# Long-before-short product pairs in an input projection, and two activation tiles moved to multiples of 64 bytes

## The chip, the core and the metric

The kernel runs on one core of one Trainium2 chip. The metric is the device time of one execution in microseconds (us), as the median of several runs. A core has a matrix engine (PE, with its weight loads shown apart as PEld), a vector engine (DVE), a scalar engine (ACT), GpSimd (POOL), a queue engine (SP) that issues DMAs here, an on-chip memory of 128 partitions (SBUF) and an accumulator memory of eight banks (PSUM), each of which holds 512 fp32 columns in every partition.

## The reference

One encoder layer on 256 tokens of width 2048. The tokens are normed and projected by one 2048 x 18432 matrix into nine parts of 2048 columns; five of them feed a bidirectional gated linear recurrence with 16 heads (group A), four feed a gated width-3 convolution (group B). Both outputs are projected together, then a gated 256-wide embedding is added, and the result is normed.

```python
hn = rmsnorm(x, norm_w)
proj = hn @ w_in                      # 2048 x 18432
q, v, f_fwd, f_bwd, z_a, b_gate, c_gate, h_b, z_b = split(proj)
o_a = hgrn2_bidirectional(silu(q), v, f_fwd, f_bwd, lb)       # chunks of 64
o_a = head_rmsnorm(o_a, hgrn_norm_w) * silu(z_a)
o_b = rmsnorm(b_gate * conv3(c_gate * h_b), conv_norm_w) * silu(z_b)
h = x + concat([o_a, o_b]) @ w_out    # 4096 x 2048
h = h + (p @ w_ple) * sigmoid(h @ w_ple_gate)                 # 2048 x 2048
return rmsnorm(h, final_norm_w)
```

Everything is fp32.

## The kernel before

**Split products.** Every operand of the four large products is written as a high part (rounded to the format fp32r, which PE multiplies in one pass here) and a low part (the rest). A product of two operands is then three products: high by high, high by low, low by high. `Stream` loads the weights as they are, in DMAs of up to 1 MB on SP's queue, into three `raw` buffers, and `split` makes the two parts in one of five `spl` buffers: ACT writes the high part (L69) and DVE the low part (L70). The splits run three buffers ahead of the products.

**The input projection.** 72 blocks, each of 256 output columns, in the order in which the program is written: first 40 for group A (eight rounds of forward gate, backward gate, q, z, v), then 32 for group B (eight rounds of c, h, b, z). A block has two accumulators `a`, one PSUM bank each (m = 0 and 1), and 16 slices `kt` of the 2048 rows. For each slice and each accumulator `gemm_part` issues a pair of products. The *long* one has 512 moving columns: the stationary operand is a high part, the moving one is the high and the low part side by side, so that both halves of the bank are written. The *short* one has 256 moving columns: the stationary operand is the low part, the moving one the high part, and it adds to the first half of the bank. With `token_major` (the z and v of group A) the stationary operand is the activation `xs` and the moving one the weights `spl`; otherwise it is the other way about. For `kt == 0` the long product goes first (L284, L285), because it starts both halves of the bank; for all later slices the short one goes first (L287) and the long one second (L288).

**What stands between the products.** While group A's blocks run, the recurrence of the round before is done on DVE, ACT and POOL, with small products on PE. These are put between two calls of `gemm_part` by `at` and `tick`, a hand-written clock that counts calls: scores and state products (`scps`, `cx`; L459, L501), outputs (`o`; L511, L512), and the transposes `ogt` of a finished head (L359), whose result ACT and DVE write to `mixa`. The last of them fall in the fourth of group B's blocks. After that nothing but pairs stands in PE's queue until the input projection ends. Group B's gated result is written to `mixb`.

**The output projection and the gate.** `gemm_tok` multiplies `mixa` and `mixb` (stationary) by `w_out` (moving) into `pa` and `pb`: for each slice and accumulator three products of 512 columns, L630 and L631 with the high part of the activations and L632 with their low part. The same function then multiplies the transposed sum `ht` by the gate's weights into `pg` (512 columns, at the end 256), and `pt` by the embedding's weights into `pp`.

**Where the tiles lie.** Pools are filled from the low end (left) and from the high end (right) of a partition. `const` is at the left with many small tiles, each rounded up to 32 bytes; `raw`, `spl` and `xs` follow it, and `ht` takes the place of `xs`. `mixa` is the first tile of the right side; the recurrence's working tiles (`ap`) and later `mixb` are placed below it. In the built program `mixa` starts at byte 196,576 of a partition and `mixb` at 163,808, both 32 past a multiple of 64, and with them all working tiles of the recurrence but a few of the smallest. `xs`, `ht` and `pt` and all `spl` buffers start at multiples of 64.

Of the kernel before, what the change touches and what calls it, by code (L numbers as in the profile page):

```python
# [8 lines left out]
F32 = mybir.dt.float32  # L9
F32R = mybir.dt.float32r  # L10
# [7 lines left out]
P = 128  # L18
D = 2048
T = 256  # L20
NKT = D // P
NH = 16
# [58 lines left out]
def tile_hymba_encoder(  # L81
# [15 lines left out]
    act, dve, pool, pe = nc.scalar, nc.vector, nc.gpsimd, nc.tensor  # L97
    out2 = out[0].rearrange("(m p) d -> p m d", p=P)

    const = ctx.enter_context(tc.tile_pool(name="const", bufs=1))  # L100
# [6 lines left out]
    xp = xctx.enter_context(tc.tile_pool(name="xp", bufs=1, side="left"))  # L107
    mctx = ExitStack()
    mixp = mctx.enter_context(tc.tile_pool(name="mixp", bufs=1, side="right"))
    mixa = mixp.tile([P, NH, 2, T], F32R, name="mixa")  # L110
    actx = ExitStack()
    ap_ = actx.enter_context(tc.tile_pool(name="ap", bufs=1, side="right"))

# [101 lines left out]
    def tick():  # L215
        now[0] += 1
        due = sorted(e for e in pend if e[0] <= now[0])
        for e in due:
            pend.remove(e)
        for e in due:  # L220
            e[2]()
# [9 lines left out]
            in1=xs[:, kt, 0, :], op0=ALU.mult, op1=ALU.subtract,  # L231
        )

    rx = const.tile([P, 2], F32, name="rx")
    rbc = const.tile([P, T], F32, name="rbc")
    rbc2 = const.tile([P, T], F32, name="rbc2")
    ss8 = const.tile([P, 2, 4], F32, name="ss8")
# [34 lines left out]
    def gemm_part(acc, w, g, token_major):  # L272
        for k in range(4):
            kt = 4 * g + k
            for m in range(2):
                a = acc[m].rearrange("p a b -> p (a b)")
                if token_major:
                    lh, ll = xs[:, kt, 0, m * P : (m + 1) * P], xs[:, kt, 1, m * P : (m + 1) * P]
                    rf, rh = w[:, k, :, :].rearrange("p s n -> p (s n)"), w[:, k, 0, :]
                else:  # L280
                    lh, ll = w[:, k, 0, m * P : (m + 1) * P], w[:, k, 1, m * P : (m + 1) * P]
                    rf, rh = xs[:, kt, :, :].rearrange("p s n -> p (s n)"), xs[:, kt, 0, :]
                if kt == 0:
                    pe.matmul(a, lhsT=lh, rhs=rf, start=True, stop=False)  # L284
                    pe.matmul(a[:, :T], lhsT=ll, rhs=rh, start=False, stop=False)  # L285
                else:
                    pe.matmul(a[:, :T], lhsT=ll, rhs=rh, start=False, stop=False)  # L287
                    pe.matmul(a, lhsT=lh, rhs=rf, start=False, stop=(kt == NKT - 1))  # L288
            tick()

    def gemm_in(c, i, token_major):
        acc = acc_in(c, i)
        for g in range(4):
            gemm_part(acc, ws.get(blocks[c, i][g]), g, token_major)
        return acc
# [21 lines left out]
    with tc.manual_schedule(engines={ENG.Activation, ENG.DVE, ENG.PE}):  # L317
        for g in range(4):
            for c in range(2):
                half, v = ws.open(ids2[c][g])  # L320
                if g == 0 and c == 0:
                    for q in range(2):
                        x_split(2 * q)
                        ws.split(half[:, 2 * q : 2 * q + 2], v[:, 2 * q : 2 * q + 2])
                        x_split(2 * q + 1)
                else:
                    if g:
                        x_split(4 * g + 2 * c)
                        x_split(4 * g + 2 * c + 1)
                    ws.split(half, v)  # L330
            for c in range(2):
                gemm_part(acc2[c], ws.parts[ids2[c][g]], g, False)
# [254 lines left out]
        act.copy(out=hi, in_=cg)  # L587
        dve.tensor_tensor(out=lo, in0=cg, in1=hi, op=ALU.subtract)

    rb = const.tile([P, 2], F32, name="rb")  # L590

    def norm_b():
        rp = psm.tile([P, 512], F32, tag="kv", name="rp")
# [70 lines left out]
    fw = gp.tile([P, D], F32, name="fw")  # L664
    nc.sync.dma_start(fw, final_norm_w.rearrange("(o d) -> o d", o=1).broadcast_to([P, D]))
    ssf = const.tile([P, 2, 5], F32, name="ssf")
    rf = const.tile([P, 2], F32, name="rf")
    dummy = const.tile([P, 2], F32, name="dummy")

    def table(func, j):  # L670

# [38 lines left out]
    for j, (c0, n) in enumerate(GCOLS):  # L710
        cs = slice(c0, c0 + n)
        if c0 % 512 == 0:
# [3 lines left out]
            for m in range(2):  # L716
                t = gp.tile([P, 512], F32, tag="pl", name=f"pl{j}_{m}", bufs=4)
# [69 lines left out]
```

## Time and profile before

| what | value |
|---|---|
| median of 3 runs | 1159.03 us (1158.61 to 1160.16) |
| the profiled execution, its own time | 1158.74 us |
| its span from first to last instruction | 1157.0 us (1.7 us lie around it) |
| PE busy | 1142.3 us (99%), 6832 products |
| DVE, ACT, POOL busy | 763.6, 639.9, 234.8 us |
| mean granted clock of PE | 0.995 |

A PE product's busy time in the profile runs from its start to a modelled end in the pipeline, and the next product starts before it. So a product's cost in a stream is the time from its start to the next one's start, which the timeline shows; the mean durations in the groups can be compared with each other only.

### The profile page before, as it was taken

The numbers are of one execution on the slowest core, as the hardware profiler recorded it, in microseconds if no ns is written. First come the engines' busy times: TensorE is split into PE (matmuls) and PEld (weight loads), VectorE is DVE, ScalarE is ACT, GpSimd is POOL, SyncE is SP. The second block draws the span as 40 slices with busy tenths as digits, with TensorE's granted clock in tenths as the row PEclk, the third lists the DMA queues.
The fourth block names the chain that finished last, engine by engine and source line by source line (L and its number), as shares of the span: only waits on it lengthen the run. The fifth ranks groups of instructions, "written<-read, shape, count | busy, mean of one in ns | idle before, by whom it ended". The sixth has DMA issues, their size and how long they took to land.

```text
span 1157.0 us, 16851 instructions
## 1 busy us (share of the span) xinstructions
PE 1142.3 (99%) x6832; PEld 981.4 (85%) x6832; DVE 763.6 (66%) x949; ACT 639.9 (55%) x889; POOL 234.8 (20%) x167
## 2 busy tenths in 40 slices
PE   8999999999999999999999999999999999999997
PEld 7878888888888888888888888888888888888886
DVE  6687777685958585966666666676666545545554
ACT  6767576666758584855544444444444334434554
POOL 1232414151414041331221221121210000000121
PEclk9999999999999999999999999999999999999999
DMA  8754545454544555455555555555557555555541
GB/s 284 301 175 153 183 163 196 152 183 146 198 167 159 174 177 181 152 178 182 183 187 184 198 191 187 182 182 184 187 190 262 183 198 180 191 204 196 197 166 74
DMA packets 31614, 214.29 MB, mean 185 GB/s; under 512 B 3504, under 2 KB 3888, under 8 KB 7088
## 3 DMA queue, kind: packets, MB, share of 16 engines
q1 hardware_dynamic: 31392, 213.14, 53.6%
q8 instruction: 53, 0.87, 0.3%
q14 instruction: 25, 0.20, 0.1%
q10 hardware_dynamic: 144, 0.08, 0.0%
HBM read 211.11 MB, written 2.10 MB: 184 GB/s over the span
## 4 chain that ended last, share of the span: by engine, by line
PE 93%; DVE 2%; DMA 2%; POOL 1%; ACT 1%; SPq 0%; issue 0%; ACTq 0%; DVEq 0%
PE a L288 41%; PE a L287 21%; PE a L284 3%; PE pa L630 3%; PE pb L630 3%; PE pb L631 3%; PE pb L632 3%; PE pa L631 3%; PE pa L632 3%; PE pg L630 3%; PE pg L631 3%; PE pg L632 3%; PE a L285 1%; DVE spl L70 1%; PE scps L459 1%; PE cx L501 1%
## 5 line engine op out<-in xcount | busy, mean ns | idle before, releaser
L70 DVE TENSOR_TENSOR spl<-raw,spl 128x1024 fp32r<-128x1024 f32 (+1 forms) x389 | 522.3, 1348 | 305.9 <-ACT spl L69 304.9
L288 PE MATMUL a<-xs,spl 128*128 128x512 f32 x1680 | 597.2, 398 | 0.0
L69 ACT CAST spl<-raw 128x1024 fp32r<-128x1024 f32 (+1 forms) x389 | 405.0, 1045 | 343.0 <-PE a L288 193.7
L287 PE MATMUL a<-xs,spl 128*128 128x256 f32 x1680 | 476.0, 283 | 0.5 <-DVE spl L70 0.3
L288 PEld LDWEIGHTS a<-xs,spl 128*128 128x128 f32 x1680 | 316.7, 189 | 73.0
L287 PEld LDWEIGHTS a<-xs,spl 128*128 128x128 f32 x1680 | 318.1, 189 | 3.7 <-DVE spl L70 1.3
L288 PE MATMUL a<-spl,xs 128*128 128x512 f32 x480 | 171.4, 401 | 2.2 <-DVE spl L70 2.2
L287 PE MATMUL a<-spl,xs 128*128 128x256 f32 x480 | 135.4, 282 | 0.0
L288 PEld LDWEIGHTS a<-spl,xs 128*128 128x128 f32 x480 | 91.0, 190 | 24.1 <-DVE spl L70 2.5
L287 PEld LDWEIGHTS a<-spl,xs 128*128 128x128 f32 x480 | 91.4, 190 | 0.7
L307 ACT COPY r<-a 128x256 f32<-128x256 f32 x112 | 40.6, 372 | 47.4 <-PE a L288 46.8
L691 POOL TENSOR_TENSOR hh<-hh,fw 128x512 f32<-128x512 f32 (+1 forms) x10 | 12.8, 1293 | 264.5 <-PE pp L632 245.0
L630 PE MATMUL pg<-spl,ht 128*128 128x512 f32 (+1 forms) x160 | 55.7, 348 | 0.0
L632 PE MATMUL pg<-spl,ht 128*128 128x512 f32 (+1 forms) x160 | 55.5, 347 | 0.0
L631 PE MATMUL pg<-spl,ht 128*128 128x512 f32 (+1 forms) x160 | 55.5, 347 | 0.0
L630 PE MATMUL pa<-spl,mixa 128*128 128x512 f32 x128 | 51.2, 400 | 0.0
L438 POOL TENSOR_TENSOR qc<-pf,ge 128x256 f32<-128x256 f32 x16 | 43.9, 2748 | 34.4 <-DVE pf L430 34.4
L631 PE MATMUL pb<-spl,mixb 128*128 128x512 f32 x128 | 50.6, 395 | 0.0
L630 PE MATMUL pb<-spl,mixb 128*128 128x512 f32 x128 | 50.6, 395 | 0.0
L632 PE MATMUL pb<-spl,mixb 128*128 128x512 f32 x128 | 50.6, 395 | 0.0
L631 PE MATMUL pa<-spl,mixa 128*128 128x512 f32 x128 | 50.6, 395 | 0.0
L632 PE MATMUL pa<-spl,mixa 128*128 128x512 f32 x128 | 50.6, 395 | 0.0
(174 smaller groups left out, 1233.7 us busy)
## 6 DMA issues: line engine op xcount, KB each, us to landing
raw<-in_w_in_dram SPq DMA_DIRECT2D x140, 1024.0 KB, 5.0
raw<-in_w_out_dram SPq DMA_DIRECT2D x32, 1024.0 KB, 4.9
raw<-in_w_gate_dram SPq DMA_DIRECT2D x12, 1024.0 KB, 4.9
raw<-in_w_gate_end_dram SPq DMA_DIRECT2D x4, 1024.0 KB, 4.9
raw<-in_w_in_dram SPq DMA_DIRECT2D x7, 512.0 KB, 8.4
xf<-in_xtok_dram SPq DMA_DIRECT2D x1, 2048.0 KB, 9.9
hh<-in_xtok_dram SPq DMA_DIRECT2D x1, 2048.0 KB, 8.8
raw<-in_w_ple_dram SPq DMA_DIRECT2D x4, 512.0 KB, 3.5
```

Of the source, the lines that this page charges most:

```text
L69: self.nc.scalar.copy(out=v[:, :, 0, :], in_=r)
L70: self.nc.vector.tensor_tensor(out=v[:, :, 1, :], in0=r, in1=v[:, :, 0, :], op=ALU.subtract)
L284: pe.matmul(a, lhsT=lh, rhs=rf, start=True, stop=False)
L285: pe.matmul(a[:, :T], lhsT=ll, rhs=rh, start=False, stop=False)
L287: pe.matmul(a[:, :T], lhsT=ll, rhs=rh, start=False, stop=False)
L288: pe.matmul(a, lhsT=lh, rhs=rf, start=False, stop=(kt == NKT - 1))
L307: act.copy(out=r, in_=acc[m][:, 1, :])
L438: pool.tensor_tensor(out=c64(dst[:, d]), in0=c64(src[:, d, :, half * P : (half + 1) * P]), in1=g.unsqueeze(3).broadcast_to([P, 2, 2, CH]), ...
L630: pe.matmul(acc[m], lhsT=lh, rhs=w[:, k, 0, :], start=(kt == 0), stop=False)
L631: pe.matmul(acc[m], lhsT=lh, rhs=w[:, k, 1, :], start=False, stop=False)
L632: pe.matmul(acc[m], lhsT=ll, rhs=w[:, k, 0, :], start=False, stop=(kt == nk - 1))
L691: pool.tensor_tensor(out=h, in0=h, in1=fw[:, cs], op=ALU.mult)
```

## The change

Two edits. The first is in `gemm_part`: the branch on `kt == 0` goes, and the long product stands first in every pair of a block, the short one second. The second moves tiles: `mixa` is declared with 8 elements (32 bytes) more than it uses, and the four tiles of two elements `rx`, `rb`, `rf` and `dummy` become slices of one tile `few` of 64 bytes, in the place where `rx` was. In the built program `mixa` then starts at byte 196,544 and `mixb` at 163,776, both multiples of 64, and all large working tiles of the recurrence do too. `raw`, `spl`, `xs` and `ht` lie 64 bytes lower than before, still at multiples of 64; `rbc` and `rbc2`, which only POOL and DVE use, are now 32 past one.

```diff
-    mixa = mixp.tile([P, NH, 2, T], F32R, name="mixa")
+
+    mixa = mixp.tile([P, NH * 2 * T + 8], F32R, name="mixa")[:, : NH * 2 * T]
+    mixa = mixa.rearrange("p (k s t) -> p k s t", k=NH, s=2)
...
-    rx = const.tile([P, 2], F32, name="rx")
+    few = const.tile([P, 16], F32, name="few")
+    rx, rb, rf, dummy = (few[:, 2 * j : 2 * j + 2] for j in range(4))
...
-                if kt == 0:
-                    pe.matmul(a, lhsT=lh, rhs=rf, start=True, stop=False)
-                    pe.matmul(a[:, :T], lhsT=ll, rhs=rh, start=False, stop=False)
-                else:
-                    pe.matmul(a[:, :T], lhsT=ll, rhs=rh, start=False, stop=False)
-                    pe.matmul(a, lhsT=lh, rhs=rf, start=False, stop=(kt == NKT - 1))
+                pe.matmul(a, lhsT=lh, rhs=rf, start=(kt == 0), stop=False)
+                pe.matmul(a[:, :T], lhsT=ll, rhs=rh, start=False, stop=(kt == NKT - 1))
...
-    rb = const.tile([P, 2], F32, name="rb")
...
-    rf = const.tile([P, 2], F32, name="rf")
-    dummy = const.tile([P, 2], F32, name="dummy")
```

PE's queue at the border of two blocks of group B shows what the first edit moves. The rows are `a` (block, round, accumulator and a running number) <- moving, stationary; before:

```order
L287 MATMUL a48_1_1_5314<-xs_149,spl179_5315 128x256
L288 MATMUL a48_1_1_5314<-xs_149,spl179_5315 128x512
L284 MATMUL a56_1_0_5402<-xs_149,spl180_5336 128x512
L285 MATMUL a56_1_0_5402<-xs_149,spl180_5336 128x256
L284 MATMUL a56_1_1_5403<-xs_149,spl180_5336 128x512
L285 MATMUL a56_1_1_5403<-xs_149,spl180_5336 128x256
L287 MATMUL a56_1_0_5402<-xs_149,spl180_5336 128x256
L288 MATMUL a56_1_0_5402<-xs_149,spl180_5336 128x512
```

The same place now (the lines after the edit are L286 for the long and L287 for the short product):

```order
L286 MATMUL a48_1_1_5314<-xs_149,spl179_5315 128x512
L287 MATMUL a48_1_1_5314<-xs_149,spl179_5315 128x256
L286 MATMUL a56_1_0_5402<-xs_149,spl180_5336 128x512
L287 MATMUL a56_1_0_5402<-xs_149,spl180_5336 128x256
L286 MATMUL a56_1_1_5403<-xs_149,spl180_5336 128x512
L287 MATMUL a56_1_1_5403<-xs_149,spl180_5336 128x256
L286 MATMUL a56_1_0_5402<-xs_149,spl180_5336 128x512
L287 MATMUL a56_1_0_5402<-xs_149,spl180_5336 128x256
```

Before, two long products follow each other at the border and two short ones between slice 0 and slice 1; now long and short alternate throughout, across the border too. The second place is the last of the small products, in the fourth of group B's blocks (`ogt15`, PE's queue); before:

```order
L288 MATMUL a64_0_1_5207<-xs_149,spl173_5151 128x512
L359 MATMUL ogt15_5248<-ident_119,ogz7_4733 128x128 x2
L287 MATMUL a64_0_0_5206<-xs_149,spl174_5172 128x256
L288 MATMUL a64_0_0_5206<-xs_149,spl174_5172 128x512
L287 MATMUL a64_0_1_5207<-xs_149,spl174_5172 128x256
```

And now:

```order
L287 MATMUL a64_0_1_5207<-xs_149,spl173_5151 128x256
L358 MATMUL ogt15_5248<-ident_119,ogz7_4733 128x128 x2
L286 MATMUL a64_0_0_5206<-xs_149,spl174_5172 128x512
L287 MATMUL a64_0_0_5206<-xs_149,spl174_5172 128x256
L286 MATMUL a64_0_1_5207<-xs_149,spl174_5172 128x512
```

The stream of pairs was taken up again with a short product; now it is with a long one. The number of products, their operands and their shapes stay, as does the order of all work on ACT, DVE, POOL and SP.

## The prediction

> **What bounds the kernel now.** I read the page's busy times and chain first, then the stages, the waits, PE's groups with shapes kept apart, and last PE's timeline, because only its starts tell what a product costs in a stream.
>
> ```profile
> span 1157.0 us, 16851 instructions
> PE 1142.3 (99%) x6832; PEld 981.4 (85%) x6832; DVE 763.6 (66%) x949; ACT 639.9 (55%) x889; POOL 234.8 (20%) x167
> PE 93%; DVE 2%; DMA 2%; POOL 1%; ACT 1%; SPq 0%; issue 0%; ACTq 0%; DVEq 0%
> ```
>
> The stages (length, then each engine's busy time, PE's granted clock, the DMA share), and PE's longest wait:
>
> ```profile
> 548.60:864.40 315.80, 315.80 (x1793) 274.47 (x1793) 207.70 (x232) 147.77 (x190) 61.51 (x42) 1.00 0.55 187
> 864.40:1051.00 186.60, 186.60 (x821) 150.49 (x820) 99.11 (x98) 77.11 (x80) 3.59 (x2) 1.00 0.58 202
> PE a L288 <- DVE spl L70: 2.2, 1, 2.2
> ```
>
> PE is the bound. In group B's stretch and in the output projection it is busy all the time at a full granted clock, with the DMA engines half idle, and its longest wait anywhere is 2.2 us. So the time can change only by what the products cost in their stream, or by new waits. The groups of PE (count, then busy us, mean ns):
>
> ```profile
> L288 PE MATMUL a<-xs,spl 128*128 128x512 f32 x1680 | 597.2, 398 | 0.0
> L287 PE MATMUL a<-xs,spl 128*128 128x256 f32 x1680 | 476.0, 283 | 0.5 <-DVE spl L70 0.3
> L631 PE MATMUL pa<-spl,mixa 128*128 128x512 f32 x128 | 50.6, 395 | 0.0
> L631 PE MATMUL pb<-spl,mixb 128*128 128x512 f32 x128 | 50.6, 395 | 0.0
> L631 PE MATMUL pg<-spl,ht 128*128 128x512 f32 x96 | 37.4, 389 | 0.0
> ```
>
> Two things stand out. A product with `mixa` or `mixb` as stationary operand lasts 395 ns; one of the same shape, from the same function and with the same moving buffers, but with `ht`, lasts 389. And the long products of the input projection have a mean of 398. The timeline (start, us, ...) turns these into prices. Output projection, then gate, each by the first and last row of an unbroken run:
>
> ```profile
> 969.66 0.39 PE L630 MATMUL pa<-spl,mixa 128*128 128x512 f32 x1
> ...
> 983.66 0.39 PE L630 MATMUL pb<-spl,mixb 128*128 128x512 f32 x1
> 1101.06 0.39 PE L631 MATMUL pg<-spl,ht 128*128 128x512 f32 x1
> ...
> 1113.98 0.39 PE L631 MATMUL pg<-spl,ht 128*128 128x512 f32 x1
> ```
>
> 60 products in 14.00 us are 233.3 ns each; 57 in 12.92 us are 226.7 ns. In the input projection I take the starts of short products, a pair (one long, one short) lying between two of them; first in the second round's c block of group B, then in one of the blocks after it:
>
> ```profile
> 551.09 0.27 PE L287 MATMUL a<-xs,spl 128*128 128x256 f32 x1
> ...
> 559.41 0.27 PE L287 MATMUL a<-xs,spl 128*128 128x256 f32 x1
> 574.18 0.28 PE L287 MATMUL a<-xs,spl 128*128 128x256 f32 x1
> ...
> 582.66 0.28 PE L287 MATMUL a<-xs,spl 128*128 128x256 f32 x1
> ```
>
> Each run has 24 pairs: 8.32 us, or 346.7 ns a pair, and 8.48 us, or 353.3 ns. These are the same instructions on the same addresses, waiting for nothing. The stream has two beats, a short one of 346.7 and a long one of 353.3 ns, 6.7 ns apart, and it keeps the beat that it is in. What it does at the places where the alternation of long and short is broken, the next rows show: the z block in which the last transposes lie, and the block borders after it.
>
> ```profile
> 538.04 0.38 PE L359 MATMUL ogt<-ident,ogz 128*128 128x128 f32 x2
> 538.18 0.48 PE L284 MATMUL a<-xs,spl 128*128 128x512 f32 x1
> ...
> 539.31 0.28 PE L287 MATMUL a<-xs,spl 128*128 128x256 f32 x1
> ...
> 543.55 0.28 PE L287 MATMUL a<-xs,spl 128*128 128x256 f32 x1
> ...
> 544.04 0.36 PE L287 MATMUL a<-xs,spl 128*128 128x256 f32 x1
> ...
> 545.18 0.28 PE L287 MATMUL a<-xs,spl 128*128 128x256 f32 x1
> ...
> 548.99 0.28 PE L287 MATMUL a<-xs,spl 128*128 128x256 f32 x1
> 560.79 0.39 PE L284 MATMUL a<-xs,spl 128*128 128x512 f32 x1
> ...
> 854.25 0.39 PE L284 MATMUL a<-xs,spl 128*128 128x512 f32 x1
> ```
>
> From 539.31 to 543.55 us 12 pairs take 4.24 us: the long beat. The next transposes (L359) interrupt the stream, it is taken up with a short product at 544.04, and from 545.18 to 548.99 us 11 pairs take 3.81 us: the short beat. It survives one block border (the run from 551.09 lies behind it) and is lost at the next: from 560.79 to 854.25 us 26 blocks take 293.46 us, 11.287 each, where 32 pairs of the short beat would be 11.093 and of the long one 11.307. So an interruption draws the beat anew, and a border may lose the short one; no border in this stretch wins it back.
>
> **The change part by part.** *Output projection.* `mixa` and `mixb` move from 32 past a multiple of 64 to a multiple, where `ht` lies. If the place is what separates 233.3 from 226.7 ns, all 4 x 32 x 2 x 3 = 768 products gain 6.7 ns: 5.1 us, all on the path, since PE has no gap there. The bounds are 0 (the place has nothing to do with it) and -5.1; a loss I exclude, since `ht` runs at such a place today. I take -5.1: moving operand, shape and function are the same on both sides of the comparison, and only the stationary tile differs. What is late next would be the splits, which DVE and ACT do in 99.1 and 77.1 of 186.6 us of that stage: there is room.
>
> The Trainium skill (TensorE: Matmul & The Clock Gate, "Step-by-step: what each phase is for") says that the engine reads weights through a port of their own, so that loading the next ones takes nothing from the running product. By that rule where `mixa` lies cannot matter and this term would be 0; the trace speaks against it as far as 395 stands against 389 ns, though no run here has yet moved a tile.
>
> *Small products.* The recurrence's tiles, stationary in `ogt`, `o` and `cx`, come to multiples of 64 too. `ogz` lies off one today and `hh` on one, and their transposes cost the same:
>
> ```profile
> L359 PE MATMUL ogt<-ident,ogz 128*128 128x128 f32 x32 | 6.1, 272 | 0.0
> L640 PE MATMUL ht<-ident,hh 128*128 128x128 f32 x32 | 4.8, 272 | 0.0
> L511 PE MATMUL o<-vt,s 128*128 128x128 f32 x64 | 12.3, 274 | 0.0
> ```
>
> I take 0; at most the 2 ns between the last row and the others, on some 200 products, which is -0.4 us.
>
> *Order, group B after the last transposes.* With strict alternation no border breaks the stream, so the beat drawn at the last `ogt` holds for the 28.5 blocks behind it, to the end of the stage. The taking-up is now by a long product. The nearest row for that is the one at 538.18 us, a long product straight behind `ogt`: what followed was the long beat. So I take the long beat. It costs 27 x (11.307 - 11.287) = 0.5 us in the blocks that run at 11.287 today, and 1.5 blocks' worth of the short beat, 1.5 x 0.21 = 0.3: +0.9 us with rounding. The other end, the short beat to the end, is 27 x (11.287 - 11.093) = -5.2 us.
>
> *Order, group A.* Here an interruption comes every few calls, and each one draws the beat again. The mean of the long products tells the present mix, between a run in the short and one in the long beat (windows 84 to 499 us, 551.1 to 559.7, and 574.2 to 582.6):
>
> ```profile
> L288 PE MATMUL a<-spl,xs 128*128 128x512 f32 x419 | 148.6, 398 | 0.0
> L288 PE MATMUL a<-xs,spl 128*128 128x512 f32 x26 | 9.1, 394 | 0.0
> L288 PE MATMUL a<-xs,spl 128*128 128x512 f32 x25 | 8.9, 399 | 0.0
> ```
>
> 398 lies four fifths of the way to the long beat. 40 blocks have 1280 pairs, 8.5 us between the two beats: all short would be -6.8 us, all long +1.7. I take 0, a mix as today's, since nothing in the rows says how `cx`, `o` and `ogt` draw with a long product behind them.
>
> *Waits.* In the blocks with moving weights (`token_major`) the long product needs the low part from DVE, and the short one, which can go ahead of that today, will be queued behind it on PE; with stationary weights it is the other way about, the long one needs ACT's part alone. The one wait of 2.2 us (v of the first round) would thus delay a short product by some 0.2 us, and start-up may delay a few more. Nobody else waits for that. The bounds are -0.5 and +0.6; I take +0.2. No DMA is moved past anything, and SP's, POOL's, ACT's and DVE's order stays.
>
> The sum on the profiled execution: 1158.74 - 5.1 + 0 + 0.9 + 0 + 0.2 = 1154.7 us. Its time is 0.3 us under the median of the runs, so 1155.0 us.
>
> **The rivals.**
>
> *The short beat holds through group B.* For it: with the borders gone, nothing is seen to end it, and the taking-up at 544.04 us did draw it. Against it: that was by a short product, and the long product at 538.18 us was followed by the long beat; but there two short ones met at slice 1, which the change removes, so that row is not a clean witness. Time: 1155.0 - 0.9 - 5.2 = 1148.9 us; with all of group A in the short beat 1142.1.
>
> *The place of `mixa` buys nothing.* The 6.7 ns could belong to something else in the stage (the writes of `mixb`'s neighbours, the accumulators). Then 1160.1 us with the long beat, 1154.0 with the short one.
>
> *Slower: long then short has a worse beat of its own.* Today the short product starts a bank's pair; then it would be the long one, with the short one on the same columns right behind it. Rows of that order exist only in slice 0, and what comes just behind them is slow:
>
> ```profile
> 573.13 0.28 PE L287 MATMUL a<-xs,spl 128*128 128x256 f32 x1
> 573.49 0.28 PE L287 MATMUL a<-xs,spl 128*128 128x256 f32 x1
> ```
>
> That is a pair in 360 ns. At 360 instead of 11.287 / 32 = 352.7 ns, 2304 pairs cost +16.8 us: 1159.0 - 5.1 + 16.8 = 1170.7 us. It decides from 352.7 + 5.1 / 2.304 = 354.9 ns a pair, where the output projection's gain is used up, and is slower beyond 355.9. Against it: in all other rows such pairs are followed by one of the two beats.
>
> **How the numbers follow.** The case of the sum 0.50, from 1148.2 (group A all short) to 1156.7 (all long); the short beat in group B 0.32; the place without effect 0.10; the worse beat 0.08. A change of 0.2%, 2.3 us, is about what a measurement of this kernel can tell from none. Faster by more are the first two, less 0.02 at the upper end of the first, and 0.04 of the third (with the short beat): 0.84. Within it is 0.02 of the first and 0.06 of the third: 0.08. Slower is the fourth: 0.08. The range goes from 1142.0 to 1157.5 us; left out are the fourth case and the third with the long beat.
>
> **What would show it.** Products with `mixa` and `mixb` start 226.7 ns apart (mean near 389), or still 233.3. Group B's blocks behind the last `ogt` take 11.31 us each, or 11.09, all alike. No short product follows a short one. I am wrong if blocks within that stretch differ, if pairs take over 355 ns, or if PE shows waits that were not there.

## The result, and the profile after

The changed kernel took 1147.72 us (median of 4 executions: 1143.09, 1144.50, 1150.94, 1151.66) against 1159.60 before; the ratio is 0.990, 95% interval 0.9876 to 0.9924. Its executions fall into two groups, near 1144 and near 1151 us, and the median of the four is the middle between them, a time that no execution took. Those of before lie within 1158.6 to 1160.2 here and within 1157.7 to 1161.5 in the later runs, without two groups. The profiled execution is one of the second group, 1150.94 us. From its groups of PE:

```profile
L629 PE MATMUL pa<-spl,mixa 128*128 128x512 f32 x128 | 49.9, 390 | 0.0
L629 PE MATMUL pb<-spl,mixb 128*128 128x512 f32 x128 | 49.8, 389 | 0.0
```

Products with `mixa` and `mixb` now have the mean of those with `ht` (395 before, 389 and 390 now). The timeline gives the stages by the starts of group B (first row), of two of its blocks 26 apart, of the output projection and of the gate:

```profile
495.67 0.48 PE L286 MATMUL a<-xs,spl 128*128 128x512 f32 x1
557.25 0.40 PE L286 MATMUL a<-xs,spl 128*128 128x512 f32 x1
851.22 0.40 PE L286 MATMUL a<-xs,spl 128*128 128x512 f32 x1
863.34 0.48 PE L628 MATMUL pa<-spl,mixa 128*128 128x512 f32 x1
1040.35 0.39 PE L628 MATMUL pp<-spl,pt 128*128 128x512 f32 x1
```

The rows of before that answer to these and were not shown above:

```profile
499.50 0.48 PE L284 MATMUL a<-xs,spl 128*128 128x512 f32 x1
866.34 0.48 PE L630 MATMUL pa<-spl,mixa 128*128 128x512 f32 x1
1048.22 0.39 PE L630 MATMUL pp<-spl,pt 128*128 128x512 f32 x1
```

The changed kernel was run once more, for its spread: 1143.15, 1143.53, 1143.54, 1145.30, 1151.27 and 1151.29 us, median 1144.42, ratio 0.989 (0.9866 to 0.9917). This time the profiled execution was one of the first group, 1143.15 us. Its same rows:

```profile
494.17 0.48 PE L286 MATMUL a<-xs,spl 128*128 128x512 f32 x1
555.21 0.39 PE L286 MATMUL a<-xs,spl 128*128 128x512 f32 x1
843.63 0.39 PE L286 MATMUL a<-xs,spl 128*128 128x512 f32 x1
855.54 0.48 PE L628 MATMUL pa<-spl,mixa 128*128 128x512 f32 x1
1032.58 0.39 PE L628 MATMUL pp<-spl,pt 128*128 128x512 f32 x1
```

> The changed kernel once more, for the spread of its executions. Theory (the beat is drawn anew in each execution at the last transposes and then kept by all of group B): times fall into two groups, near 1144 and near 1151 us, and a profile shows group B's blocks all at 11.09 us in an execution of the first group, all at 11.31 in one of the second. Rival (the spread has another source, such as the start of the program or the DMAs): times lie anywhere between, and the blocks' time does not go with them.

Differences of these rows give the stages in us:

| execution | start-up and group A | group B | a block of group B | output projection |
|---|---|---|---|---|
| before, 1158.74 | 499.5 | 366.8 | 11.287 | 181.9 |
| after, 1150.94 | 495.7 | 367.7 | 11.307 | 177.0 |
| after, 1143.15 | 494.2 | 361.4 | 11.093 | 177.0 |

32 pairs take 11.307 us in the long beat and 11.093 in the short one, to the third digit. So group B ran wholly in the long beat in one execution and wholly in the short one in the other: the same program, one beat, kept for 28 blocks. The expected two groups of times are there, and the blocks go with them. That the beat is drawn at the last transposes, as the theory also has it, is not what the traces show; "Where is the beat decided?" below comes to that. (`tick` is called after each slice, not after each call of `gemm_part` as the text ahead of the prediction has it.)

The trace keeps whole nanoseconds, where the timeline prints 10. Read so, the long beat is a pattern of three pairs, 346, 358 and 356 ns from one short product to the next, over and over: 20 ns more than three pairs of the short beat. A pair of the short beat, 346.7 ns, is just the sum of what its two products cost in the gate's uniform runs, 226.7 and 120.0 ns from start to start.

### The profile page after: what moved, and what is told of

Read it like the earlier page. It is cut to its first block, busy times and chain, and to the rows that moved or that the text cites. A ratio compares the mean times of both kernels' runs of the same rounds, so it can differ in the third digit from the quotient of the medians.

```text
span 1149.2 us, 16855 instructions
## 1 busy us (share of the span) xinstructions
PE 1135.1 (99%) x6832; PEld 982.7 (86%) x6832; DVE 764.2 (67%) x949; ACT 640.3 (56%) x889; POOL 234.7 (20%) x167
## 4 chain that ended last, share of the span: by engine, by line
PE 93%; DVE 2%; DMA 2%; POOL 1%; ACT 1%; SPq 0%; issue 0%; ACTq 0%; DVEq 0%
PE a L286 43%; PE a L287 22%; PE pg L630 3%; PE pg L628 3%; PE pg L629 3%; PE pa L628 3%; PE pa L630 3%; PE pb L628 3%; PE pb L630 3%; PE pa L629 3%; PE pb L629 3%; DMA raw<-in_w_in_dram 1%; PE scps L458 1%; DVE spl L70 1%; PE cx L500 1%; DMA xf<-in_xtok_dram 1%
## 5 line engine op out<-in xcount | busy, mean ns | idle before, releaser
L286 PE MATMUL a<-xs,spl 128*128 128x512 f32 x1792 | 638.3, 400 | 1.7 <-DVE xs L231 1.7
L287 PE MATMUL a<-xs,spl 128*128 128x256 f32 x1792 | 504.0, 281 | 0.0
L286 PEld LDWEIGHTS a<-xs,spl 128*128 128x128 f32 x1792 | 337.5, 188 | 81.5 <-ACT spl L69 2.0
L287 PEld LDWEIGHTS a<-xs,spl 128*128 128x128 f32 x1792 | 339.7, 190 | 0.4 <-DVE spl L70 0.4
L286 PE MATMUL a<-spl,xs 128*128 128x512 f32 x512 | 180.4, 396 | 2.4 <-DVE spl L70 2.4
L287 PE MATMUL a<-spl,xs 128*128 128x256 f32 x512 | 144.1, 281 | 0.0
L286 PEld LDWEIGHTS a<-spl,xs 128*128 128x128 f32 x512 | 96.7, 189 | 24.7 <-DVE spl L70 2.7
L287 PEld LDWEIGHTS a<-spl,xs 128*128 128x128 f32 x512 | 97.6, 191 | 0.0
L629 PE MATMUL pb<-spl,mixb 128*128 128x512 f32 x128 | 49.8, 389 | 0.0
L630 PE MATMUL pb<-spl,mixb 128*128 128x512 f32 x128 | 49.8, 389 | 0.0
L628 PE MATMUL pb<-spl,mixb 128*128 128x512 f32 x128 | 49.8, 389 | 0.0
```

The source lines that it names most:

```text
L286: pe.matmul(a, lhsT=lh, rhs=rf, start=(kt == 0), stop=False)
L287: pe.matmul(a[:, :T], lhsT=ll, rhs=rh, start=False, stop=(kt == NKT - 1))
L628: pe.matmul(acc[m], lhsT=lh, rhs=w[:, k, 0, :], start=(kt == 0), stop=False)
L629: pe.matmul(acc[m], lhsT=lh, rhs=w[:, k, 1, :], start=False, stop=False)
L630: pe.matmul(acc[m], lhsT=ll, rhs=w[:, k, 0, :], start=False, stop=(kt == nk - 1))
```

## The experiments

**One edit at a time.** First the moved tiles with the old order of pairs:

```diff
-                pe.matmul(a, lhsT=lh, rhs=rf, start=(kt == 0), stop=False)
-                pe.matmul(a[:, :T], lhsT=ll, rhs=rh, start=False, stop=(kt == NKT - 1))
+                (the branch on kt == 0 as before; the rest of the change stays)
```

> The kernel before with the tiles moved and the old order of the pairs. Theory (the two edits pay apart from each other): pa and pb start 226.7 ns apart instead of 233.3, 768 x 6.7 = 5.1 us less, and group B's blocks stay at 11.287 us because their borders are broken as before: 1154.5 us from 1159.6, with little spread between executions. Group A's draws may come out otherwise, since the recurrence's tiles moved too: up to 2 us either way. Rival (the place of mixa buys nothing, the output projection got its beat in another way): 1159.6, with 233.3 ns.

Measured: 1151.58 to 1154.48 us, median 1152.48 against 1160.17, ratio 0.994 (0.9927 to 0.9955). Its timeline, with the starts of two of group B's blocks 26 apart, of the output projection and of the gate; the last two rows are a q and a z block of group A:

```profile
561.30 0.39 PE L287 MATMUL a<-xs,spl 128*128 128x512 f32 x1
854.76 0.39 PE L287 MATMUL a<-xs,spl 128*128 128x512 f32 x1
866.85 0.47 PE L632 MATMUL pa<-spl,mixa 128*128 128x512 f32 x1
1043.88 0.39 PE L632 MATMUL pp<-spl,pt 128*128 128x512 f32 x1
99.99 0.40 PE L287 MATMUL a<-xs,spl 128*128 128x512 f32 x1
111.10 0.39 PE L287 MATMUL a<-spl,xs 128*128 128x512 f32 x1
```

The output projection is 177.0 us long, as after, and group B's blocks are 11.287, as before: these 4.9 us are the place's, and the broken borders alone fix group B. The median fell by 2.8 us more than that. One part is seen: the q block took 11.11 us, where the same block took 11.30 before, and from the third round on each round of group A is 0.2 us shorter; a likely reason is that the recurrence's tiles moved too and its products hand the stream on in another state, but no run has that alone. The profiled execution, 1154.48 us, is the slowest of the five and does not show the rest: its start-up and group A together took 500.2 us, against 499.5 before, because its first two rounds took 1.8 us longer, with a wait of 1.6 us for `kx` where before has one of 0.5.

Then the new order with the tiles where they were (the diff's `gemm_part` alone):

> The kernel before with the new order of the pairs and the tiles where they were. Theory: pa and pb at 233.3 ns; strict alternation keeps the beat drawn at the last transposes for all of group B, the long one (11.307 us a block, group B 0.9 us longer than before) or the short one (11.093, 5.2 shorter), and the draw differs from execution to execution: two groups of times about 6 us apart, near 1156 and 1149.5. Rival (the draws of the changed kernel come from the moved tiles, not from the order): all executions alike, near 1160.

Measured: 1147.86 once, 1153.65 to 1155.28 five times, median 1154.50 against 1160.17, ratio 0.995 (0.9927 to 0.9967). The profiled execution took 1153.65 us:

```profile
493.84 0.48 PE L283 MATMUL a<-xs,spl 128*128 128x512 f32 x1
555.15 0.40 PE L283 MATMUL a<-xs,spl 128*128 128x512 f32 x1
849.13 0.40 PE L283 MATMUL a<-xs,spl 128*128 128x512 f32 x1
861.24 0.48 PE L626 MATMUL pa<-spl,mixa 128*128 128x512 f32 x1
1043.11 0.39 PE L626 MATMUL pp<-spl,pt 128*128 128x512 f32 x1
```

The output projection keeps its 181.9 us. Group B takes 367.4 us in blocks of 11.307, the long beat, and start-up with group A takes 493.8, which is 5.7 us less than before. So the new order paid in group A, in an execution in which it cost 0.6 us in group B. The rival (all executions near 1160) is out: five times lie 4.9 to 6.5 us under the median of before and one 12.3 under it. The two groups lie 1.5 us lower than expected; start-up and group A are 1.8 us shorter here than in the changed kernel's 1150.94.

**Is it the place, and of which operand?** All in one kernel: `mixa` 16 bytes past a multiple of 64, `mixb` 4, `xs`, `ht` and `pt` 32:

```diff
+    gap = xsp.tile([P, 8], F32, tag="gap", name="gap")
...
-    mixa = mixp.tile([P, NH * 2 * T + 8], F32R, name="mixa")[:, : NH * 2 * T]
+    mixa = mixp.tile([P, NH * 2 * T + 8], F32R, name="mixa")[:, 4 : NH * 2 * T + 4]
...
-            mixb = bp.tile([P, NH, 2, T], F32R, name="mixb")
+            mixb = bp.tile([P, NH * 2 * T + 16], F32R, name="mixb")[:, 1 : NH * 2 * T + 1]
+            mixb = mixb.rearrange("p (k s t) -> p k s t", k=NH, s=2)
```

> The changed kernel with tiles put off multiples of 64 on purpose: mixa 16 bytes past one, mixb 4, xs, ht and pt 32; spl stays on one. Theory (a stationary operand off a multiple of 64 costs its product 6.7 ns, a moving one nothing): pa and pb at 233.3 ns, pg at 233.3 and its 256-column form at 126.7 instead of 120.0, pairs with xs stationary (z and v of group A) 360 ns instead of 346.7; pairs with xs moving unchanged, blocks of group B at 11.09 or 11.31 us: 5.1 + 3.5 + 6.8 = 15 us over the changed kernel, 1159 or 1166. Rival (the moving operand's place counts as well): pairs of group B 360 ns or more, 24 us on top, 1183 to 1190. Second rival (place buys nothing): 1144 or 1151, as the changed kernel.

Measured: 1151.49 us (one execution). Its groups of PE:

```profile
L631 PE MATMUL pb<-spl,mixb 128*128 128x512 f32 x128 | 50.6, 396 | 0.0
L631 PE MATMUL pa<-spl,mixa 128*128 128x512 f32 x128 | 50.4, 394 | 0.0
L631 PE MATMUL pg<-spl,ht 128*128 128x512 f32 x96 | 38.0, 395 | 0.0
L631 PE MATMUL pg<-spl,ht 128*128 128x256 f32 x64 | 18.0, 281 | 0.0
```

And its timeline, a z block of group A with `xs` stationary (the first two rows), then 26 blocks of group B with `xs` moving:

```profile
108.97 0.40 PE L287 MATMUL a<-spl,xs 128*128 128x512 f32 x1
120.27 0.40 PE L287 MATMUL a<-spl,xs 128*128 128x512 f32 x1
557.48 0.39 PE L287 MATMUL a<-xs,spl 128*128 128x512 f32 x1
845.91 0.39 PE L287 MATMUL a<-xs,spl 128*128 128x512 f32 x1
```

`ht` off its multiple brings the gate's 512-column products to 395 ns, which `mixa` and `mixb` had before, and the output projection loses its gain at 4 bytes and at 16. Group B's blocks are 11.093 us with `xs` 32 bytes off: a moving operand's place costs nothing. My theory was too wide in one point. It wanted 6.7 ns on every product; the 256-column ones, at 281 ns against 283 in the gate of before, pay nothing, and the z block pays 0.21 us (11.30 instead of 11.093), 6.6 ns a pair and not 13.3. A block in the long beat is as long (11.307), so the length alone does not tell the two apart. The pairs do: they go 350 and 357 ns in turn here, and not 346, 358, 356, and it is so in the seven rounds behind the first, each with its q block at 11.09. So the gate shows that only the long product pays, and the z blocks agree. That is why the kernel took 1151.5 us, with group B in the short beat, and not 1159.

**What makes the two beats?** Three orders of the same products. In `grouped8` each call of `gemm_part` issues its 8 long products and then its 8 short ones; in `llss` each slice issues long, long, short, short:

```diff
-            for m in range(2):
+            for long, m in ((True, 0), (True, 1), (False, 0), (False, 1)):
...
-                pe.matmul(a, lhsT=lh, rhs=rf, start=(kt == 0), stop=False)
-                pe.matmul(a[:, :T], lhsT=ll, rhs=rh, start=False, stop=(kt == NKT - 1))
+                if long:
+                    pe.matmul(a, lhsT=lh, rhs=rf, start=(kt == 0), stop=False)
+                else:
+                    pe.matmul(a[:, :T], lhsT=ll, rhs=rh, start=False, stop=(kt == NKT - 1))
```

> The changed kernel, but each call of gemm_part issues its 8 long products first and then its 8 short ones. Theory (the long beat needs long and short products that alternate one by one): 8 long ones at 226.7 and 8 short ones at 120.0 as in the gate's uniform runs, 2773 ns for 8 pairs, group B's blocks 11.09 us in every execution: 1143 us with less than 1 us of spread. Rival (the long beat comes from short products on whose start the next weight load has little room): the runs of short products keep it, blocks between 11.09 and 11.31, 1144 to 1151 us, and more than 1 us of spread.

> The changed kernel, but each slice issues long, long, short, short (accumulators 0, 1, 0, 1). Theory (alternation one by one makes the long beat): two of a kind in a row leave only the short beat or a mix of both; group B's blocks 11.09 to 11.2 us, 1143 to 1147 us. Rival (the long beat comes from a short product that writes into the accumulator that the product just before it wrote): here none does, so blocks at 11.09 in every execution and 1143 us. Second rival (any change between lengths can draw the long beat): two groups of times as in the changed kernel, 1144 and 1151.

In the third, long and short alternate one by one as after the change, but the short one mostly writes into the other accumulator than the long one before it:

```diff
+    CROSS = [(1, 0, 0), (0, 0, 1), (1, 1, 0), (0, 1, 1), (1, 0, 1), (0, 0, 0), (1, 1, 1), (0, 1, 0)]   # long?, slice, m
...
```

> The changed kernel, long and short still alternating one by one, but in 12 of 16 slices a short product writes into the other accumulator than the long one just before it (two slices as long 0, short 1, long 0, short 1, long 1, short 0, long 1, short 0). Theory (the two beats come from the alternation of lengths, whatever the accumulator): both beats appear again, undisturbed stretches at 346.7 or 353.3 ns a pair, and executions differ: 1143 to 1152 us. Rival (the long beat comes from a short product on the accumulator of the product before it): group B at 11.09 us a block but for the four slices in the old order, at most 11.14, in all executions: 1143 to 1145 us with little spread.

Measured: `grouped8` 1147.09 to 1148.35 us; `llss` 1145.29 to 1146.55; `cross_bank` 1143.53, 1143.58, 1144.38 and 1151.65, 1151.83, 1152.11. Starts of two of group B's blocks 26 apart, in `grouped8`:

```profile
558.23 0.40 PE L288 MATMUL a<-xs,spl 128*128 128x512 f32 x1
848.73 0.40 PE L288 MATMUL a<-xs,spl 128*128 128x512 f32 x1
```

In `llss`:

```profile
556.86 0.40 PE L287 MATMUL a<-xs,spl 128*128 128x512 f32 x1
846.67 0.40 PE L287 MATMUL a<-xs,spl 128*128 128x512 f32 x1
```

And in the profiled `cross_bank`, which took 1152.11 us:

```profile
558.44 0.40 PE L296 MATMUL a<-xs,spl 128*128 128x512 f32 x1
852.40 0.40 PE L296 MATMUL a<-xs,spl 128*128 128x512 f32 x1
```

Blocks of 11.173, 11.147 and 11.306 us. Which accumulator a short product writes has no part in it: `cross_bank` shows both groups of times and the long beat to the digit. Alternation one by one does: without it there is one block time in all 28 blocks, and the four executions of each kernel lie 1.3 us apart instead of 8. But the expected 11.093 did not come. These two orders cost something themselves, 3.4 ns for each long, long, short, short (11.147 less 11.093 over 16) and 20 ns for each run of 8 and 8 (11.173 over 4). It is not a price of each change of length, since the short beat changes at every product and pays none. So alternation one by one can be cheaper than either grouping, or dearer, by its beat. The rival of `grouped8`, little room for the weight load when a short product starts, is not settled: its ranges (blocks between 11.09 and 11.31, over 1 us of spread) fit what came. In the trace the short products of a run start 114 to 120 ns apart, no slower than in the gate, and the extra time lies on the first five long ones behind them, at 228 to 236 ns instead of 226.7.

**What does a break in the alternation do?** From group B's second round on, the fifth slice of each block was disturbed, in eight ways in turn: 0 not at all, 1 long long short short, 2 long short short long, 3 short long short long, 4 four and four, 5 to 7 one or two spare products of 128 columns. A second kernel had the same in another sequence.

> The changed kernel, in which from group B's second round on the fifth slice of each block is disturbed in one of eight ways in turn: 0 not at all, 1 long long short short, 2 long short short long, 3 short long short long, 4 two slices as four long and four short, 5 a spare two-pass product of 128 columns ahead of it, 6 a spare one-pass product of 128 columns, 7 two of these (the spare products' results are not used). Theory (the beat is set where strict alternation is broken and kept until the next such place): the beat changes only at the disturbed slices, never at kind 0, and a kind leads to the same beat each time or keeps the one that was there. Rival (something outside the stream sets it, the splits or the DMAs): changes at undisturbed places too, and no kind with a fixed outcome. Time: 28 disturbances of at most 0.3 us on 1144 to 1151, 1145 to 1156.

> The same eight disturbances of group B's blocks as in the first probe, in another sequence (2 2 2 6 6 6 2 6 2 1 1 2 5 5 6 7 7 2 3 3 6 4 2 2 1 6 5 2 from the second round on), so that each meets both beats. In the first probe 2 (long short short long) and 6 (a spare one-pass product) turned the long beat into the short one three and four times out of as many; 3, 4 and 7 turned the short into the long. Theory A (a disturbance shifts the stream's phase by a fixed amount, and some shifts lead to the short beat from both): 2 or 6 or both keep the short beat when they meet it, blocks with 2 after 2 at 11.09 us. Theory B (a disturbance swaps the beats): 2 after 2 and 6 after 6 alternate between 11.31 and 11.09. Time 1144 to 1152.

Times 1150.58 and 1152.59 us (one execution each). The starts of short products 15 pairs apart, behind the disturbance, in three blocks in a row of the first kernel, with kinds 1, 2 and 3:

```profile
607.17 0.28 PE L312 MATMUL a<-xs,spl 128*128 128x256 f32 x1
...
612.47 0.28 PE L312 MATMUL a<-xs,spl 128*128 128x256 f32 x1
618.44 0.28 PE L312 MATMUL a<-xs,spl 128*128 128x256 f32 x1
...
623.64 0.28 PE L312 MATMUL a<-xs,spl 128*128 128x256 f32 x1
629.57 0.28 PE L312 MATMUL a<-xs,spl 128*128 128x256 f32 x1
...
634.87 0.28 PE L312 MATMUL a<-xs,spl 128*128 128x256 f32 x1
```

The same in the second kernel, in a block with kind 2 that came in the long beat and one with kind 2 that came in the short one:

```profile
552.66 0.28 PE L313 MATMUL a<-xs,spl 128*128 128x256 f32 x1
...
557.96 0.28 PE L313 MATMUL a<-xs,spl 128*128 128x256 f32 x1
812.45 0.28 PE L313 MATMUL a<-xs,spl 128*128 128x256 f32 x1
...
817.75 0.28 PE L313 MATMUL a<-xs,spl 128*128 128x256 f32 x1
```

5.30 us are the long beat, 5.20 the short one. In the first kernel kind 1 left the long beat, kind 2 made it short and kind 3 long again, all three times that the sequence came round, and no block changed its beat away from its disturbance. That is the first theory's first half: the beat changes where alternation is broken and nowhere else. The second half fell. In the second kernel kind 2 left the long beat long in five blocks (the first pair of rows is one), made it short in two, kept the short one in one and made it long in two (the second pair of rows). So neither a fixed outcome nor a plain swap: what a break does depends on where in its own pattern the stream is when it comes. No break that always ends in the short beat was found.

That it depends on the place in the pattern can be read from the pairs in whole nanoseconds. Where kind 2 met the long beat, the short one followed each time that the pair ahead of the disturbance was one of about 356 ns (five of five), and the long one each time that it was one of 346 or 358 (five of five). (The short beat comes in two forms, with pairs that are all alike or with 345 and 348 ns in turn, and there the form is the place.) Over both kernels 12 combinations of a kind and a place came more than once, 44 breaks in all, and none led to two different beats. So the outcome looked like a draw because the place was not known.

**Where is the beat decided?** The same holds across executions. The lengths of group A's rounds in us, in six profiled executions whose group A alternates one by one and whose tiles lie as in the changed kernel:

| execution | rounds three to eight | group B's undisturbed blocks |
|---|---|---|
| `after`, 1150.94 | 60.61, 60.63, 61.36, 60.62, 61.36, 60.62 | 11.307 |
| `cross_bank`, 1152.11 | 60.61, 60.63, 61.36, 60.62, 61.36, 60.62 | 11.306 |
| `draw_probe2`, 1152.59 | 60.61, 60.63, 61.36, 60.62, 61.36, 60.62 | (disturbed) |
| `after_again`, 1143.15 | 60.62 in all six | 11.093 |
| `draw_probe`, 1150.58 | 60.62 in all six | (disturbed) |
| `twos_b`, 1144.26 | 60.62 in all six | (other order) |

There are two courses, and within each the distances between PE's starts agree with those of `after` or `after_again` to 2 ns from the third round to the z block of group B's first round, through all interruptions (in `twos_b` to the end of group A). In `cross_bank` the q block of the fifth round and the v block two blocks on start at:

```profile
280.19 0.40 PE L296 MATMUL a<-xs,spl 128*128 128x512 f32 x1
...
302.81 0.40 PE L296 MATMUL a<-spl,xs 128*128 128x512 f32 x1
```

These are 22.62 us, the long beat, as in the same round of `after` (its rows stand in the next section). So an interruption does not draw: it leads on from the state in which it finds the stream. In these six, what differs between executions is settled before the third round, which starts near 131 us, and the beat of group B follows from it.

**A version with one time.** `llss` in group B alone, group A as after the change:

> The changed kernel with long long short short in group B alone (group A alternates one by one as in the changed kernel). In the run with that order everywhere group B's blocks took 11.15 us each and the executions lay within 1.3 us. Theory (two and two has one beat, in every execution): 32 blocks at 11.15, between the changed kernel's two cases (11.09 and 11.31), so 1143.3 + 32 x 0.06 = 1145.2 us with the better draws of group A and up to 1148 with the worse, spread at most 3 us, all of it from group A. Rival (two and two only happened to draw well there): blocks at 11.2 or more in some executions, times up to 1152.

Measured: 1144.26, 1145.94, 1146.00 and 1146.07 us, ratio 0.988 (0.9869 to 0.9897). Its blocks:

```profile
554.89 0.40 PE L292 MATMUL a<-xs,spl 128*128 128x512 f32 x1
844.70 0.40 PE L292 MATMUL a<-xs,spl 128*128 128x512 f32 x1
```

11.147 us, as expected, and the spread of the four is 1.8 us; group B's blocks were seen in one of them, so that the rest comes from elsewhere is likely but not shown. The ten executions of the changed kernel have a median of 1144.9 and a mean of 1146.8 us; this one has 1145.6 as its mean. It is 5.7 us under the mean of the changed kernel's poor group and 1.7 over that of the good one. The two kernels were not timed side by side, so on the middle of the times they are not told apart; what it removes, as far as four executions tell, is the spread.

## Why the prediction was right, and where it was not

1147.7 us lies in the range (1142.0 to 1157.5), as does every single execution, and it was faster, as 0.84 said. 1155.0 itself was 7 us too high: the case that was ranked first, the long beat in group B, came in four executions of ten, and even these took 1151 us, because group A gained as well. The three stages of the table account for the profiled times to 0.1 us: 3.8 less, 0.8 more and 4.9 less in one execution, 5.3, 5.5 and 4.8 less in the other.

- *Output projection, -5.1.* Measured -4.9 (181.9 to 177.0 us), with the tiles moved alone as well, and undone by moving them off again. By the reading of the Trainium skill in the prediction (TensorE: Matmul & The Clock Gate, "Step-by-step: what each phase is for": weights have a read port of their own) the term would have been 0; for products of 512 columns it is not. The passage speaks of the port and not of addresses, and no run here tells why the place counts; the weight loads themselves last 188 ns in the profile before and after. For products of 256 columns, at 281 and 283 ns, the place cost nothing.
- *Order, group B, +0.9 or -5.2.* Both sizes were right: +0.8 in the profiled execution (366.8 to 367.7 us, blocks of 11.307), -5.5 in the other one. The wrong step was to set them against each other with 0.50 and 0.32. They are not two ways in which the kernel can turn out but two courses that executions of the same kernel take: of the changed kernel's ten executions six were near 1144 us and four near 1151, so the median falls between the cases or in either. The sentence "it keeps the beat that it is in" was read from one execution; how the first beat comes about across executions could not be read there, since in the kernel before the borders break the alternation and its blocks end up alike.
- *Order, group A, 0.* This term was mis-sized: start-up and group A took 3.8 us less in one profiled execution and 5.3 in the other, 5.7 with the order alone. The step that failed is "an interruption comes every few calls, and each one draws the beat again". The q and z blocks of each round but the first have no interruption, so what was argued for group B's borders holds for them too, and the interruptions do not draw: the two courses run through them unchanged. Rounds three to eight gave 2.5 us in the one execution and 4.0 in the other; the remaining 1.3 lie in start-up and the first two rounds, whose waits differ between executions. The starts of a q block and of the v block two blocks on, before:

```profile
97.76 0.40 PE L284 MATMUL a<-xs,spl 128*128 128x512 f32 x1
...
120.34 0.39 PE L284 MATMUL a<-spl,xs 128*128 128x512 f32 x1
```

And in the changed kernel's 1150.94 us, the same blocks and those of a later round:

```profile
97.04 0.39 PE L286 MATMUL a<-xs,spl 128*128 128x512 f32 x1
...
119.22 0.39 PE L286 MATMUL a<-spl,xs 128*128 128x512 f32 x1
...
279.00 0.40 PE L286 MATMUL a<-xs,spl 128*128 128x512 f32 x1
...
301.62 0.40 PE L286 MATMUL a<-spl,xs 128*128 128x512 f32 x1
```

  22.58 us before, where the borders between the blocks are broken and the time stays near the long beat's; 22.18 now, the short beat in both blocks, and 22.62 in the two rounds that were in the long beat. Such pairs of blocks were there in seven of the eight rounds; in the first round's q block other small products (`rps`) stand between.
- *Small products 0, waits +0.2.* The longest wait went from 2.2 to 2.4 us, on the same block of the first round. Nothing larger was seen of either in that execution.
- *Rivals.* The worse beat of long before short does not exist: group B has the old two beats and no other. It was priced on one pair read as 360 ns from starts printed to 10 ns; in whole nanoseconds that pair took 353, and pairs of 358 stand in every long beat, so it was no sign of a beat of its own. That the place buys nothing is refuted by the two kernels that moved tiles. The short beat through group B is, by their times, what six of ten executions show; one of these was profiled.

**Open.** What sends executions of one program on different courses was not found; it lies before the third round, and no run changed that stretch alone. The two longest waits of PE behind the start-up do not sort the executions: they were 1.8 and 1.6 us in `after_again` and in `cross_bank`, which took different courses. Nor does a stretch of some 3.4 us at a granted clock of 0.50, near 65 to 71 us, which `after`, `draw_probe2` and `twos_b` have and the other three of the table do not. Nor is it shown why a stream that alternates two lengths has two beats: the choice of accumulator is ruled out, the lengths' alternation is needed, and the rest is not known.

## What to carry to other kernels

Price a product in a dense PE stream by the distance of starts in the timeline, in several stretches: two distances for the same instructions tell of a mode that the stream is in, and the question is then where it is decided and what breaks it. One pair is not enough, since a mode can be a pattern of several. One profiled execution shows one course; before a mode is forecast as a case, ask whether executions share it, and look at the spread of the times. Put stationary tiles of fp32r that feed products of 512 columns at multiples of 64 bytes; it takes a few bytes of padding, and the tile next to it tells what it is worth.

## What the runs showed of the hardware

A stationary operand 4, 16 or 32 bytes past a multiple of 64 brought products of 512 columns from 389 or 390 to 394 to 396 ns, or from 226.7 to 233.3 ns from start to start at 32; with 256 columns it cost nothing, and a moving operand 32 bytes off cost nothing. A stream of 512- and 256-column products in strict alternation ran at 346.7 or at 353.3 ns a pair, held either for 28 blocks of 32 pairs, and took one or the other in different executions of the same program. The slower one is a pattern of pairs of 346, 358 and 356 ns. Where the alternation was broken, the beat that followed went with the kind of the break and the place in the pattern at which it came, without exception in 44 breaks.
